# Layer 0 of a two-layer diffusion trunk: two of 24 modulation chunks made by ScalarE and GpSimd instead of TensorE

## The chip, the cores and the metric

The kernel runs on one core of one Trainium2 chip. Its time is the device time of one execution in microseconds (us), and a version's time is the median of its runs. TensorE (PE) multiplies matrices, VectorE (DVE), ScalarE (ACT) and GpSimd (POOL) work on tiles of 128 partitions, and SyncE (SP) issues the loads. Each engine runs its own list of instructions in a fixed order and waits on semaphores.

## The reference

Two streams of 256 tokens with 2048 features pass through two layers: the latent stream h, modulated by c, and the context stream hc, modulated by c_ctx. Everything is float32. What matters here is layer i = 0, with a pooling mixer:

```python
ml = (silu_c @ w_mod[i] + b_mod[i]).reshape(B, 6, 1, D)
mc = (silu_cc @ w_mod[i] + b_mod[i]).reshape(6, 1, 1, D)
...
a_lat = modulate(rms_norm(h, norm1_g[i]), ml[:, 0], ml[:, 1])
y_lat = pool_mix(a_lat, ...)
h = h + ml[:, 2] * y_lat
h = h + ml[:, 5] * conv_ffn(modulate(rms_norm(h, norm2_g[i]), ml[:, 3], ml[:, 4]), ...)
```

The same is done for hc with mc. `silu_c @ w_mod[i]` is a product of one vector per stream with a matrix of 2048 x 12288, so the weights are read for two columns only. `ml[:, 5]` and `mc[:, 5]`, the second gate, multiply what the FFN adds, and are needed last of the six.

## The kernel before

**Data.** Features lie on partitions, 128 at a time (16 tiles k), and the tokens of both streams side by side in 512 columns. A matrix product in float32 is made as three passes of a rounded type: high part times high part, high times low, low times high. ScalarE makes the high part of a weight tile (L173, a cast) and VectorE the low part (L175, a subtraction).

**Modulation.** The 12288 columns of layer 0 are 24 chunks of 512; chunk 4*which + q holds quarter q of vector number `which`, so 20 to 23 are the second gate. `mod_pe` (L231) makes a chunk on TensorE in four steps; each step loads two tiles of 512 KB, and the matmuls of L247 use the weights as the moving operand and the two condition columns as the stationary one (32 columns wide, four such groups side by side). Then ScalarE copies the result out of PSUM (L263, `modev`), four transposes (L270, `modt`) turn it, VectorE reduces it (L272) and adds the bias (L221). Chunks 22 and 23 (`LATER`) are made otherwise, on VectorE, during the FFN (`mod_pairs`): weight times condition plus sum (L315), and at the end a transpose within blocks of 32 (L325), a reduction (L326) and a small matmul that adds up the quarters (L205, `quarter_sum`). A result of chunk 20 or later is first read in the FFN's down product (L980).

**Stages.** The mixer works in four groups g of four feature tiles, and the first part of the FFN is interleaved with it: `partial(g)` multiplies the tiles of group g with the first eight column blocks f of the gate and up weights (L780 to L782, tiles `cg` and `cu`), and VectorE adds each product to a sum (L796, `part`). The shift of `modulate` goes in as a small product `pwg` or `pwu` of the raw weights with the shift columns `sh` (L759), which is copied out, transposed (L801) and reduced. The operand of group g, `Ad`, is made by ScalarE (L713) and VectorE (L714) from the mixer's output `hl`, `hc`, which is made from the mixer's matmuls `pm` (L637 to L639) by ScalarE (L701) and VectorE (L703); the sum of squares for the second norm is collected beside it (L356, L362; `n2q`, `n2acc`).

**Order.** `partial(g)` calls `between(half)` 32 times, before and inside each product. There `need(n)` advances the generator `mods()`, one step of a modulation chunk at a time (for group g the chunks g, 4+g, 8+g, 16+g, 12+g; after the last group 20 and 21), and `next(mix)` advances the mixer of the next group. In group 3 there is no mixer left; at its half 3 the second norm is closed (`n2.diagonal`, L406 to L414), at half 5 spread over all partitions (L422, `n2b`) and copied by ScalarE (L843), and from then on VectorE normalises (L438) and makes the operands A of the FFN proper (L449), and corrects the sums (L514).

**Loads.** All weight loads go through one queue on SP, one behind the other in the order of the program. A load takes one of a few rooms of 512 KB (`stage`): the one that the program freed first. It waits until all readers of the room's tile before are done, and everything behind it in the queue waits too. Three PSUM banks named "d" rotate among the products, the transposes and the small matmuls.

Of the kernel before, what the change touches and what calls it, by code (L numbers as in the profile page):

```python
# [10 lines left out]
F32 = mybir.dt.float32  # L11
F32R = mybir.dt.float32r
AF = mybir.ActivationFunctionType
ALU = mybir.AluOpType
AX = mybir.AxisListType
PSUM = bass.MemoryType.PSUM

P = 128
# [15 lines left out]
LEAD = 18  # L34
RATE = 20
PMAX = 30

NRH = 3
LATER = (22, 23)

LENT = {(2, 31): range(4, 12), (3, 6): range(8, 12), (3, 15): ()}

# [17 lines left out]
def kernel(ctx: ExitStack, tc: tile.TileContext, xT, cxT, wmod, wg, wu, wd, wp,  # L60
                         wq, wv, wo, vec, cc, rope, inv, strips, out):
    nc = tc.nc
# [34 lines left out]
    sc2 = main.tile([P, KT, 2], F32, name="sc2")  # L97
# [21 lines left out]
    def used(ts):  # L119

        for t, _ in ts:
            freed[keeper.pop(id(t))[0]] = tick()

    def lend(ks):

        for k in ks:
            if k not in rooms and k in freed:
                freed[k] = tick()
        rooms[:] = [r for r in rooms if r < 0 or r in ks] + [k for k in ks if k not in rooms]
# [15 lines left out]
    def load(src, cols, name):  # L145

        ts = []
        for j in range(0, cols, 1024):
            n = min(1024, cols - j)
            t = stage(f"{name}_{j}")  # L150
            with ExitStack() as behind:
                for ins in fetched[-1:] if in_turn else ():
                    behind.enter_context(tc.issue_after(ins))
                fetched.append(nc.sync.dma_start(t[:, :n], src(j, j + n)).ins)
            ts.append((t, n))
        return ts
# [31 lines left out]
    both = (0, 1)  # L188
# [40 lines left out]
    prod_of = []  # L229
# [250 lines left out]
    with ExitStack() as ph0:  # L480
        p0 = ph0.enter_context(tc.tile_pool(name="p0", bufs=1, reuse_waits="tile"))
        f0 = ph0.enter_context(tc.tile_pool(name="f0", bufs=6, reuse_waits="tile"))
# [11 lines left out]
        def act_tile(name, dt):  # L494
            return f0.tile([P, 2, 512], dt, tag="act", bufs=7, name=name)
# [61 lines left out]
        with ExitStack() as phs:  # L557
# [37 lines left out]
            def mods():  # L595

                for g in range(4):
                    for w in (0, 1, 2, 4):
                        yield from mod_pe(0, 4 * w + g, sc, f0)
                    yield from mod_pe(0, 12 + g, sc, f0)  # L600
                    shifts(g)
                for q in range(4):
                    if 20 + q not in LATER:
                        yield from mod_pe(0, 20 + q, sc, f0)

            pump0 = mods()
            done = [0]

            def need(n):
                while done[0] < n:  # L610
                    next(pump0, None)
                    done[0] += 1
# [212 lines left out]
            for g in range(4):  # L825
                if g < 3:
                    lend((range(8, KT), [*range(12, KT), *range(4)], range(8))[g])
                mix = mixer(g + 1) if g < 3 else None
                todo = [20 * g + 20 + n for n in STEPS] if g < 3 else []
                last = [14]  # L830
                F = {}
                rstd = n2.acc

                def between(half):
                    n = 20 * g + LEAD + (RATE if g < 3 else 19 - 4 * len(LATER)) * (half + 1) // 32
                    need(min(n, 20) if g == 0 and half == 4 else n)
                    if (g, half) in LENT:
                        lend(LENT[g, half])
                    if g == 3 and half == NRH:
                        n2.diagonal()  # L840
                        need(20 * g + 21)
                    if g == 3 and half == NRH + 2:
                        nc.scalar.copy(rstd, n2.spread_all(behind_of))  # L843
                        late_norm.append(rstd)
                    if todo and done[0] > todo[0] and half >= last[0] + 2:
                        last[0] = half
                        todo.pop(0)
                        next(mix)
                    k = (half - NRH) // 2 - 1
                    if g == 3 and 0 <= k < 12 and (half - NRH) % 2 == 0:  # L850
                        normalise(0, 3, h_of, both, rstd, f0, range(k, k + 1), keep=F)
                    if g == 3 and half == 24:
                        EARLY[NC] = late(NC, (0,))[0]
                    if g == 3 and half == 26:
                        spare = act_tile("nrm_spare", F32)
                        for j in range(2):
                            scaled[12 + j] = scale(0, 3, h_of, both, rstd, f0, 12 + j,
                                                   spare[:, j].rearrange("p (s t) -> p s t", s=2))
                    if g == 3 and half == 27:
                        for j in (14, 15):  # L860
                            scaled[j] = scale(0, 3, h_of, both, rstd, f0, j)

                partial(g, shs[g % 2], between)
                for n in todo:
                    need(n)
                    next(mix)
            need(97 - 4 * len(LATER))
            behind_of.clear()
            vector_behind.clear()
            nbank[0] = 0  # L870
# [833 lines left out]
```

## Time and profile before

| what | value |
|---|---|
| time, median of 3 runs | 3016.59 us |
| lowest and highest run | 3014.61 and 3019.01 us |
| profiled execution: its span | 3014.1 us |
| profiled execution: its own time | not listed apart from the span |
| PE busy | 2959.5 us, 98% of the span |
| DVE, ACT, POOL busy | 66%, 46%, 27% |
| DMA queues, share of 16 engines | 57.2% |
| mean of what HBM moved | 186 GB/s |

The profile is that of one execution, whose span is 2.5 us below the median and 0.5 us below the lowest run. Busy time counts instructions, not register or semaphore work. The stage of the change lies in the first 400 us: group 1 runs from about 155 to 245 us, group 2 from 245 to 335, group 3 from 335 to 400. A row of a timeline gives start, duration, engine, line, operation, result<-operands, count, and in brackets the idle time before it and what ended that.

### The profile page before, as it was taken

The page shows a single profiled execution, that of the slowest core. Times are in us where ns is not written, and L with a number is a line of the kernel's source. Part 1 is how long each engine was busy: PE and PEld are TensorE (multiplying, and loading weights), DVE is VectorE, ACT ScalarE, POOL GpSimd, SP SyncE. Part 2 cuts the span into 40 slices and gives each one's busy share as a digit, 9 for nine tenths or more (in the row PEclk, how much of TensorE's full clock was granted, in tenths as well). Part 3 has the DMA queues.
Part 4 walks back from the last instruction along what each step waited for, and adds up shares of the span by engine and source line. Part 5 has one row for each costly group of instructions (what it writes and reads, how often), then busy time and mean ns, then how long its engine had stood idle before and what let it go on. Part 6 is the DMA issues. An engine that isn't in the chain of part 4 may idle for free.

```text
span 3014.1 us, 40862 instructions
## 1 busy us (share of the span) xinstructions
PE 2959.5 (98%) x15068; PEld 2412.1 (80%) x15068; DVE 1998.0 (66%) x2895; ACT 1375.1 (46%) x2231; POOL 809.4 (27%) x782
## 2 busy tenths in 40 slices
PE   5999999999999999999999999999999999999998
PEld 3666678888888888888888887878788888888887
DVE  4455799657484866748576657484778666666666
ACT  4433454433333233333434534353546666566665
POOL 0000006212213031220314002020003665566665
PEclk9999999999999999999999999999999999999999
DMA  9798555565574847557472334342356566555553
GB/s 395 292 366 308 179 184 159 181 209 187 169 230 145 254 141 220 185 175 231 141 246 90 121 99 128 99 131 98 100 174 201 177 199 192 189 182 189 181 194 116
DMA packets 178935, 561.80 MB, mean 186 GB/s; under 512 B 17712, under 2 KB 22576, under 8 KB 178736
## 3 DMA queue, kind: packets, MB, share of 16 engines
q1 hardware_dynamic: 178736, 559.19, 57.2%
q8 instruction: 119, 1.95, 0.3%
q14 instruction: 80, 0.66, 0.1%
HBM read 557.03 MB, written 2.10 MB: 186 GB/s over the span
## 4 chain that ended last, share of the span: by engine, by line
PE 91%; DVE 3%; DMA 3%; POOL 1%; issue 1%; ACT 1%; SPq 0%; DVEq 0%; ACTq 0%; POOLq 0%
PE g L1186 5%; PE u L1186 5%; PE d L969 5%; PE d L967 5%; PE d L968 5%; PE d L1239 4%; PE g L902 4%; PE g L904 4%; PE g L903 4%; PE u L902 4%; PE u L904 4%; PE u L903 4%; PE g L1189 3%; PE u L1189 3%; PE d L1243 2%; PE k L1369 2%
## 5 line engine op out<-in xcount | busy, mean ns | idle before, releaser
L315 DVE SCALAR_TENSOR_TENSOR macc<-wm,sc,macc 128x512 f32<-128x512 f32 (+1 forms) x420 | 381.9, 941 | 71.5 <-DMA wm<-wmod 70.2
L981 POOL TENSOR_TENSOR hl<-hl,dy 128x256 f32<-128x256 f32 x160 | 154.1, 963 | 984.6 <-ACT dy L980 984.4
L1255 POOL TENSOR_TENSOR hl<-hl,dy 128x256 f32<-128x256 f32 x320 | 323.3, 1046 | 214.2 <-ACT dy L1253 212.0
L980 ACT ACTIVATE dy<-d,modT 128x256 f32<-128x256 f32 x320 | 133.4, 470 | 193.4 <-PE d L969 168.8
L981 POOL TENSOR_TENSOR hc<-hc,dy 128x256 f32<-128x256 f32 x160 | 133.3, 833 | 0.0
L1253 ACT ACTIVATE dy<-d,modT 128x512 f32<-128x512 f32 x160 | 104.5, 684 | 43.7 <-PE d L1243 41.2
L175 DVE TENSOR_TENSOR wd_2l<-wd,wd_2h 128x1024 fp32r<-128x1024 f32 (+1 forms) x44 | 55.9, 1275 | 91.3 <-ACT wd_2h L173 90.4
L175 DVE TENSOR_TENSOR wd_3l<-wd,wd_3h 128x1024 fp32r<-128x1024 f32 (+1 forms) x44 | 53.8, 1241 | 80.2 <-ACT wd_3h L173 79.1
L1341 POOL TENSOR_TENSOR rk<-rk,rp 128x256 f32<-128x256 f32 x16 | 15.1, 946 | 316.5 <-DVE rk L1340 223.4
L247 PE MATMUL mod<-wm,sc 128*32 128x512 f32 x704 | 88.8, 624 | 7.5 <-DMA wm<-wmod 7.4
L175 DVE TENSOR_TENSOR wd_1l<-wd,wd_1h 128x1024 fp32r<-128x1024 f32 (+1 forms) x44 | 54.8, 1248 | 47.8 <-ACT wd_1h L173 47.6
L411 POOL TENSOR_TENSOR n2v<-n2v,minus_half 128x4 f32<-128x4 f32 x1 | 1.0, 1011 | 316.0 <-DVE n2v L410 316.0
L173 ACT CAST wd_1h<-wd 128x1024 fp32r<-128x1024 f32 (+1 forms) x44 | 45.3, 1032 | 67.0 <-PE u L903 41.0
L175 DVE TENSOR_TENSOR wd_0l<-wd,wd_0h 128x1024 fp32r<-128x1024 f32 (+1 forms) x44 | 54.4, 1244 | 25.8 <-ACT wd_0h L173 25.0
L536 ACT ACTIVATE sg<-g 128x512 f32<-128x512 f32 x43 | 27.2, 632 | 95.9 <-DVE g L533 95.8
L1436 ACT ACTIVATE sb<-sb,nm 128x512 f32<-128x512 f32 x64 | 46.1, 721 | 52.8 <-DVE nm L1432 52.2
L967 PE MATMUL d<-act,wd_1h 128*128 128x512 f32 x172 | 67.0, 390 | 0.8 <-ACT dy L980 0.8
L967 PE MATMUL d<-act,wd_2h 128*128 128x512 f32 x172 | 67.0, 390 | 0.0
L968 PE MATMUL d<-act,wd_2h 128*128 128x512 f32 x172 | 66.9, 389 | 0.0
L968 PE MATMUL d<-act,wd_1h 128*128 128x512 f32 x172 | 66.9, 389 | 0.0
L967 PE MATMUL d<-act,wd_0h 128*128 128x512 f32 x172 | 66.9, 389 | 0.0
L969 PE MATMUL d<-act,wd_2l 128*128 128x512 f32 x172 | 66.7, 390 | 0.1
(1799 smaller groups left out, 9252.8 us busy)
## 6 DMA issues: line engine op xcount, KB each, us to landing
wm<-wmod SPq DMA_DIRECT2D x384, 512.0 KB, 6.5
wd<-wd SPq DMA_DIRECT2D x168, 512.0 KB, 4.4
wg<-wg SPq DMA_DIRECT2D x156, 512.0 KB, 4.7
wu<-wu SPq DMA_DIRECT2D x156, 512.0 KB, 4.7
wv<-wv SPq DMA_DIRECT2D x32, 512.0 KB, 4.2
wk<-wq SPq DMA_DIRECT2D x32, 512.0 KB, 3.8
wq<-wq SPq DMA_DIRECT2D x32, 512.0 KB, 3.8
wo<-wo SPq DMA_DIRECT2D x31, 512.0 KB, 4.0
```

Of the source, the lines that this page charges most:

```text
L175: low_of[:] = [eng.tensor_tensor(lo[:, :n], t[:, :n], hi[:, :n].bitcast(F32), op=ALU.subtract).ins]
L315: nc.vector.scalar_tensor_tensor(acc[s], v, sc2[:, k, s : s + 1], acc[s], op0=ALU.mult, op1=ALU.add)
L902: nc.tensor.matmul(ps, hi[:, c : c + P], xh, start=(k == 0), stop=False)
L903: nc.tensor.matmul(ps, hi[:, c : c + P], xl, start=False, stop=False)
L904: ins = nc.tensor.matmul(ps, lo[:, c : c + P], xh, start=False, stop=(k == KT - 1))
L967: nc.tensor.matmul(ps, hi[:, o : o + P], xh, start=(i == 0), stop=False)
L968: nc.tensor.matmul(ps, hi[:, o : o + P], xl, start=False, stop=False)
L969: ins = nc.tensor.matmul(ps, lo[:, o : o + P], xh, start=False, stop=(i == n - 1))
L981: nc.gpsimd.tensor_tensor(h_of(s)[:, k, :], h_of(s)[:, k, :], y[:, s], op=ALU.add)
L1186: nc.tensor.matmul(ps, hi[:, c : c + P], flat(B[k]), start=(k == 0), stop=False)
L1189: nc.tensor.matmul(ps[:, T:], lo[:, c : c + P], B[k][:, 0], start=False, stop=(k == KT - 1))
L1255: nc.gpsimd.tensor_tensor(hl[:, k, :], hl[:, k, :], y[:, q], op=ALU.add)
```

## The change

Chunks 20 and 21 leave `mods()`. A new generator `mod_beside` makes them in 16 pieces, eight for each chunk. A piece loads one tile of 512 KB (two feature tiles k of 512 columns) through the same queue and rooms; ScalarE multiplies each half with the condition of each stream (four instructions of 128x512; for stream 1 into a scratch tile `modp`, for stream 0 in place into the weight tile), and GpSimd adds the four products to the sums `beside`. Of a chunk's first half ScalarE writes the sums itself. So there are 64 instructions on ScalarE (L621, L624, L625) and 60 on GpSimd (L626, L627). After the last piece of a chunk VectorE makes two transposes and two reductions (L633, L634, tiles `modu` and `modr`), and two halves later the quarter sum goes to TensorE (L207, `modt_20s`, `modt_21s`), issued behind the last product, and VectorE adds the bias. `BESIDE` sets piece i at half 40 + 4i, counted 32g + half: chunk 20 lies in group 1 from half 8 on and in group 2 at halves 0 and 4, chunk 21 in group 2 from half 8 on and in group 3 at halves 0 and 4. The 16 loads of the two chunks in group 3 are gone there, and `need` counts eight steps fewer. The sums' tile serves later as the spare tile of the norm. Line numbers grow: L154 becomes L156, L173 L175, L247 L249, L759 L795, L780 L816, L796 L832.

```diff
+ASIDE = (20, 21)
+BESIDE = {40 + 4 * i: i for i in range(16)}
...
-                    if 20 + q not in LATER:
+                    if 20 + q not in LATER + ASIDE:
                         yield from mod_pe(0, 20 + q, sc, f0)
...
+            def mod_beside(todo):
+
+                acc = act_tile("beside", F32)
+                BESIDE_ACC.append(acc)
+                for ch in todo:
+                    for piece in range(8):
+                        g, j = divmod(2 * piece, 4)
+                        ts = load(lambda a, b: wmod[0, ch, g, :, 512 * j + a : 512 * j + b], 1024, f"wm0_{ch}_{piece}")
+                        for i in range(2):
+                            v = ts[0][0][:, 512 * i : 512 * i + 512]
+                            k = 2 * piece + i
+                            if k == 0:
+                                for s in both:
+                                    nc.scalar.activation(acc[:, s], v, AF.Copy, scale=sc2[:, k, s : s + 1])
+                                continue
+                            w = f0.tile([P, 512], F32, tag="t2", name=f"modp_{ch}_{k}")
+                            nc.scalar.activation(w, v, AF.Copy, scale=sc2[:, k, 1:2])
+                            nc.scalar.activation(v, v, AF.Copy, scale=sc2[:, k, 0:1])
+                            nc.gpsimd.tensor_tensor(acc[:, 1], acc[:, 1], w, op=ALU.add)
+                            nc.gpsimd.tensor_tensor(acc[:, 0], acc[:, 0], v, op=ALU.add)
+                        used(ts)
+                        if piece == 7:
+                            r = st.tile([P, 16, 2], F32, bufs=1, name=f"modr_0_{ch}")
+                            for s in both:
+                                t = f0.tile([P, 512], F32, tag="t2", name=f"modu{s}_0_{ch}")
+                                nc.vector.transpose(t, acc[:, s])
+                                nc.vector.tensor_reduce(out=r[:, :, s], in_=t.rearrange("p (k r) -> p k r", r=32),
+                                                        axis=AX.X, op=ALU.add)
+                            beside_sums.append((ch, r))
+                        yield
...
-                    n = 20 * g + LEAD + (RATE if g < 3 else 19 - 4 * len(LATER)) * (half + 1) // 32
+                    n = 20 * g + LEAD + (RATE if g < 3 else 19 - 4 * len(LATER + ASIDE)) * (half + 1) // 32
...
+                    if 32 * g + half in BESIDE:
+                        next(beside)
+                    if 32 * g + half - 6 in BESIDE and beside_sums:
+                        ch, r = beside_sums.pop()
+                        finish_mod(0, ch, both, quarter_sum(r, 2, f"modt_0_{ch}", prod_of))
...
-                        spare = act_tile("nrm_spare", F32)
+                        spare = BESIDE_ACC[0]
...
-            need(97 - 4 * len(LATER))
+            need(97 - 4 * len(LATER + ASIDE))
```

The order of the instructions changes with it. On SP, where group 1 passes into group 2, the queue before reads as follows (`wm_14` and `wm_3` are the modulation weights of chunks 14 and 3 on their way to TensorE, `wcg` and `wcu` weights of the gate and up products):

```order
155 L154 DMA wm_14_2_0_2088<-wmod 128x1024
156 L154 DMA wm_14_2_1024_2090<-wmod 128x1024
157 L154 DMA wm_14_3_0_2106<-wmod 128x1024
158 L624 DMA inv_2418<-inv 128x256
159 L154 DMA wm_14_3_1024_2108<-wmod 128x1024
160 L154 DMA wm_3_0_0_2137<-wmod 128x1024
161 L154 DMA wm_3_0_1024_2139<-wmod 128x1024
162 L154 DMA wm_3_1_0_2155<-wmod 128x1024
163 L154 DMA wm_3_1_1024_2157<-wmod 128x1024
```

The same place of the queue now, with what the loads wait for:

```order
162 L156 DMA wm_20_6_0_2151<-wmod 128x1024 [waits DMAHW1_49,PE_49]
163 L156 DMA wm_14_2_0_2170<-wmod 128x1024 [waits DMAHW2_49]
164 L156 DMA wm_14_2_1024_2172<-wmod 128x1024 [waits DMAHW3_49]
165 L156 DMA wm_14_3_0_2188<-wmod 128x1024 [waits DMAHW4_49,Pool_49]
166 L156 DMA wm_14_3_1024_2190<-wmod 128x1024 [waits DMAHW5_49,PE_49]
167 L156 DMA wm_3_0_0_2219<-wmod 128x1024 [waits DMAHW6_49]
168 L156 DMA wm_3_0_1024_2221<-wmod 128x1024 [waits DMAHW7_49]
169 L156 DMA wm_20_7_0_2223<-wmod 128x1024 [waits DMAHW0_49]
170 L156 DMA wm_3_1_0_2256<-wmod 128x1024 [waits DMAHW1_49]
```

Pieces 6 and 7 of chunk 20 stand in the queue, and the first tile of `wm_14_3` takes the room of piece 5 (`wm_20_5`), so it waits for GpSimd; before, the queue had no wait on GpSimd here.

On ScalarE, between the mixer's last outputs of group 1 (`pz`) and the operands of group 2 (`Ad`), now:

```order
179 L624 ACTIVATE modp_10_2007<-wm_20_5_0_2005,sc_82 128x512
180 L175 CAST wcg_0h_2143<-wcg_0_0_2139 128x1024
181 L358 ACTIVATE n2q_1980<-hc 128x256
182 L624 ACTIVATE modp_11_2012<-wm_20_5_0_2005,sc_82 128x512
183 L737 ACTIVATE pz_2036<-pm_2_2023,gbi_1707,gsc_1706 128x256 x2
184 L625 ACTIVATE wm_20_5_0_2005<-wm_20_5_0_2005,sc_82 128x512 x2
185 L358 ACTIVATE n2q_2041<-hl 128x256
186 L737 ACTIVATE pz_2058<-pm_3_2045,gbi_1707,gsc_1706 128x256 x2
187 L749 ACTIVATE Ad_2105<-hl,modT_18_2078 128x256
```

The four instructions on `wm_20_5` (L624, L625) are new in this list, and the others stand as before.

On PE, ahead of `pwg` of group 2, before (the end of `cg_2`'s product, then `pwg`):

```order
775 L782 MATMUL cg_2_2141<-Ad_2059,wcg_0bl_2078 128x512
776 L780 MATMUL cg_2_2141<-Ad_2064,wcg_0bh_2077 128x512
777 L781 MATMUL cg_2_2141<-Ad_2064,wcg_0bh_2077 128x512
778 L782 MATMUL cg_2_2141<-Ad_2064,wcg_0bl_2078 128x512
779 L759 MATMUL pwg_0_2167<-wcg_0_0_2069,sh_213 32x256
```

And now, with `modr_20` the reduced sums of chunk 20:

```order
774 L818 MATMUL cg_2_2242<-Ad_2134,wcg_0bl_2148 128x512
775 L249 MATMUL mod_3_2218<-wm_3_1_1024_2258,sc 32x512 x2
776 L249 MATMUL mod_3_2218<-wm_3_1_0_2256,sc 32x512 x2
777 L249 MATMUL mod_3_2218<-wm_3_0_1024_2221,sc 32x512 x2
778 L249 MATMUL mod_3_2218<-wm_3_0_0_2219,sc 32x512 x2
779 L207 MATMUL modt_20s<-modr_20_2235,quad 128x32
780 L795 MATMUL pwg_0_2275<-wcg_0_0_2139,sh_213 32x256
```

The matmuls of chunk 3 stood ahead of `cg_2` before; the quarter sum of chunk 20 is directly ahead of `pwg`.

On VectorE in group 3, now, from the sums' correction to the first operand A (`modT_21` is the bias add behind the quarter sum of chunk 21, which stands on PE between `n2b` and `pwg`):

```order
383 L832 TENSOR_TENSOR part_662<-part_662,cg_2_3113 128x512
384 L516 TENSOR_TENSOR part_604<-part_604,n2acc 128x512
385 L516 TENSOR_TENSOR part_633<-part_633,n2acc 128x512
386 L516 TENSOR_TENSOR part_662<-part_662,n2acc 128x512
387 L633 STREAM_TRANSPOSE modu_0_21_3107<-beside 128x512
388 L633 STREAM_TRANSPOSE modu_0_21_3110<-beside 128x512
389 L440 SCALAR_TENSOR_TENSOR nrm_3123<-hl,modT_16_521,n2acc 128x256
390 L440 SCALAR_TENSOR_TENSOR nrm_3123<-hc,modT_16_521,n2acc 128x256
391 L634 TENSOR_REDUCE modr_21_3106<-modu_0_21_3107 128x16
392 L634 TENSOR_REDUCE modr_21_3106<-modu_0_21_3110 128x16
393 L451 SCALAR_TENSOR_TENSOR A_0_3_3126<-nrm_3123,modT_12_647,A_0_3_3126 128x256 x2
394 L223 TENSOR_TENSOR modT_21_3140<-modt_21s,vt_70 32x8 x4
```

The transposes and reductions of chunk 21 are new there, and stand behind three corrections that wait for `n2b`.

More of the change, by code (lines that the diff above doesn't have):

```diff
@@ L602, in mods @@
                 for q in range(4):
-                    if 20 + q not in LATER:
+                    if 20 + q not in LATER + ASIDE:
                         yield from mod_pe(0, 20 + q, sc, f0)
+            def mod_beside(todo):
[27 more added lines that the diff above has]
+                        yield
+            BESIDE_ACC = []
+            beside_sums = []
+            beside = mod_beside(ASIDE)
             pump0 = mods()
```

## The prediction

> **What bounds the kernel now.** I read the page first, then the busy times by stage, then the chain of waits around the edges of the groups, where the change puts its work. The page's lines of engines and of the chain that ended last:
>
> ```profile
> PE 2959.5 (98%) x15068; PEld 2412.1 (80%) x15068; DVE 1998.0 (66%) x2895; ACT 1375.1 (46%) x2231; POOL 809.4 (27%) x782
> ```
>
> ```profile
> PE 91%; DVE 3%; DMA 3%; POOL 1%; issue 1%; ACT 1%; SPq 0%; DVEq 0%; ACTq 0%; POOLq 0%
> ```
>
> TensorE is the bound: 98% busy, 91% of the chain. So work taken from it counts in full, if nothing new makes it wait. Busy times by stage, in the columns span, PE, PEld, DVE, ACT, POOL (each us and instructions), granted clock, DMA share, GB/s. The rows are group 1, group 2 and group 3:
>
> ```profile
> 155.00:245.00 90.00, 87.18 (x523) 55.92 (x522) 50.99 (x105) 32.49 (x60) 0.00 (x0) 1.00 0.90 330
> 245.00:335.00 90.00, 86.24 (x498) 57.10 (x497) 54.78 (x113) 32.37 (x60) 0.00 (x0) 0.98 0.83 304
> 335.00:400.00 65.00, 64.37 (x374) 43.32 (x374) 49.57 (x108) 36.25 (x72) 1.01 (x1) 1.00 0.51 168
> ```
>
> GpSimd stands nearly idle in all three and ScalarE is half free, so the averages speak for the change. Group 3, from which the work goes, has TensorE full (64.37 of 65). But the averages hide two things: groups 1 and 2 are where the loads are densest (0.90 and 0.83 of the DMA engines), and TensorE waits there only at the group's edge.
>
> **What leaves TensorE.** All matmuls and transposes of chunks 20 and 21 lie between 354 and 400 us:
>
> ```profile
> L247 PE MATMUL mod<-wm,sc 128*32 128x512 f32 x64 | 7.9, 600 | 0.0
> ```
>
> ```profile
> L270 PE MATMUL modt<-ident,modev 128*128 128x128 f32 x8 | 1.2, 271 | 0.0
> ```
>
> That is 9.1 us by durations, which overlap at their ends. A run of 32 such matmuls of another chunk, as the timeline has it, takes 3.64 from start to end:
>
> ```profile
> 239.86 3.64 PE L247 MATMUL mod<-wm,sc 128*32 128x512 f32 x32
> ```
>
> Two of them are 7.3, and with some 1.0 of the transposes I take 8.3 us. The stage is full, so I count -8.3. Their sixteen loads leave a queue that is half idle (0.51) and count as nothing; the one wait that may go with them is this:
>
> ```profile
> PE cu L782 <- DVE wcu_4l L175: 0.5, 1, 0.5
> ```
>
> It hangs on a weight tile that stands behind those loads, so -0.5. What is late next there is VectorE, with 49.57 of 65 us, below TensorE.
>
> **What is added, by price.** The nearest rows for ScalarE's products, GpSimd's sums, VectorE's transposes and reductions and the quarter sums:
>
> ```profile
> L263 ACT COPY modev<-mod 128x512 f32<-128x512 f32 x21 | 12.3, 584 | 45.7 <-PE mod L247 45.6
> ```
>
> ```profile
> L362 POOL TENSOR_TENSOR n3q<-n3q,n3q 128x512 f32<-128x512 f32 x11 | 15.8, 1434 | 10.7 <-ACT n3q L356 7.4 <-issue 3.0
> ```
>
> ```profile
> L325 DVE STREAM_TRANSPOSE modu<-macc x36: 659/682/705, 480.4 to 1617.3; 128x512 f32<-128x512 f32 x36
> L326 DVE TENSOR_REDUCE modr<-modu x36: 633/662/675, 482.8 to 1619.2; 128x16 f32<-128x512 f32 x36
> ```
>
> ```profile
> L205 PE MATMUL modt_22s<-modr,quad x4: 178/226/274, 486.8 to 1619.4; 128*128 128x32 f32 x2, 128*128 128x16 f32 x2
> ```
>
> A piece costs ScalarE 4 x 0.58 = 2.3 us, or less where steps overlap (below); GpSimd 4 x 1.43 = 5.7; a chunk's end costs VectorE 2 x 0.68 + 2 x 0.66 = 2.7 and TensorE 0.25. ScalarE's 64 (37 us) and GpSimd's 60 (86 us) spread over some 180 us and fit. So it is not the load of an engine that decides but four places at which someone waits for them.
>
> **Place one: from group 1 to group 2.** The chain of waits there, before, then the queue of SP, and ScalarE's list (the run of 32 matmuls above is TensorE there, chunk 14):
>
> ```profile
> 243.82 10.47 DMA wcu<-wu
> 254.31 1.06 ACT wcu_0h L173
> ...
> 257.27 1.09 PE pwg L759 x16
> ...
> 258.80 0.23 PE cg L781
> ```
>
> ```profile
> 229.76 14.02 SPq L154 DMA_DIRECT2D wm<-wmod  x7
> 243.82 1.31 SPq L154 DMA_DIRECT2D wcu<-wu  x2
> ```
>
> ```profile
> 237.89 0.58 ACT L263 COPY modev<-mod 128x512 f32<-128x512 f32 x1
> 238.35 1.04 ACT L701 ACTIVATE pz<-pm,gbi,gsc 128x256 f32<-128x256 f32 x2
> ```
>
> SP's queue stood still for 14 us, because rooms were not free; loads at the edge land late, and `pwg` ran at 257.27, held by a load. Now the queue also holds a load of chunk 20 in about every eighth place, and the first tile of step 3 of chunk 14 waits for GpSimd's sums on piece 5. ScalarE's four products of that piece stand behind the `modev` copy, among a cast and the `pz`: they end at about 239, 240.7, 242.1 and 242.6, so GpSimd, at 1.43 each, ends the last sum at about 245.0. Starts 0.46 apart (237.89 and 238.35) bring Ad 4 x 0.46 = 1.8 us later. Behind the load that waits, the queue holds the other tile of step 3, two tiles of chunk 3 and piece 7. Landing times and spacing:
>
> ```profile
> wm<-wmod SPq DMA_DIRECT2D x384, 512.0 KB, 6.5
> wd<-wd SPq DMA_DIRECT2D x168, 512.0 KB, 4.4
> ```
>
> ```profile
> 185.00:200.00 15.00, 15.00 (x98) 9.92 (x98) 4.99 (x12) 3.28 (x4) 0.00 (x0) 1.00 1.02 404
> ```
>
> A queue that has run empty lands its first load after 4.4 to 6.5 us; I take 5, nearer the lower, since nothing is ahead of it. At 404 GB/s 512 KB take 1.3 us. So step 3 of chunk 14 lands from 250.0 to 251.3 (TensorE had read it by 243.5), piece 7 at 250.0 + 4 x 1.3 = 255.2. Then a product 0.6, four sums 5.7, the chunk's end on VectorE 2.7 and the quarter sum 0.25: 264.5. The quarter sum stands directly ahead of `pwg`, so `pwg` runs at 264.5 in place of 257.27: +7.2, and 6.6 to 8.7 by the two landing times. TensorE itself has, behind the late tiles (251.3), half of chunk 14 and half of chunk 3 (0.9 each), some 22 products at 0.23 and four transposes to do, 251.3 + 1.8 + 5.1 + 0.6 = 258.8, so these delays, the late Ad among them, lie inside the 7.2. At the lower end, were piece 7 there early, 258.8 - 257.3 = 1.5 is left. Behind the quarter sum on TensorE everything is queued, and VectorE and ScalarE wait for its products.
>
> **Place two: the start of group 3.** Rows of TensorE, ScalarE and VectorE there:
>
> ```profile
> 344.81 1.02 PE L422 MATMUL n2b<-n2d,ones 128*128 128x512 f32 x2
> 345.76 1.09 PE L759 MATMUL pwg<-wcg,sh 128*32 128x256 f32 x16
> ```
>
> ```profile
> 345.87 0.59 ACT L843 COPY n2acc<-n2b 128x512 f32<-128x512 f32 x1 [3.26 <-PE n2b L422]
> ```
>
> ```profile
> 346.49 0.48 DVE L438 SCALAR_TENSOR_TENSOR nrm<-hl,modT,n2acc 128x256 f32<-128x256 f32 x1
> ```
>
> ```profile
> 347.29 1.89 DVE L514 TENSOR_TENSOR part<-part,n2acc 128x512 f32<-128x512 f32 x3
> ```
>
> Today `pwg` follows `n2b` at once. Now the quarter sum of chunk 21 stands between them, and its operand comes from VectorE behind three corrections that themselves need the copy of `n2b`: copy until 346.5, corrections 1.89, two transposes 1.3, two `nrm` 0.9, two reductions 1.3, the quarter sum 0.25, that is 352.1. So +6.3 on a TensorE that had nothing to wait for. GpSimd's last sum, on a piece whose load stands well ahead, would be ready at about 347.7 (products from 341.4, then four sums), before the transposes; if it were 2 us later, that would show in full. Nothing hides this wait but matmuls that the program put behind it.
>
> **Place three: from group 2 to group 3.** The chain there ran through ScalarE and VectorE:
>
> ```profile
> 325.45 0.92 ACT pz L701 x2
> 326.37 0.94 ACT wcg_0h L173
> 327.34 1.22 DVE wcg_0l L175
> ```
>
> Three products of a piece (1.4 us) stand in ScalarE's list ahead of the first Ad: +1.4, between 0 (if the low part is later anyway) and 1.8, a whole piece.
>
> **Place four: VectorE beside a busy GpSimd.** VectorE is nearly full in the last third of each mixer, first group 1, then group 2:
>
> ```profile
> 200.00:215.00 15.00, 15.00 (x101) 9.01 (x103) 14.62 (x29) 7.38 (x13) 0.00 (x0) 1.00 0.95 323
> ```
>
> ```profile
> 290.00:305.00 15.00, 15.00 (x93) 10.83 (x96) 13.48 (x27) 6.51 (x10) 0.00 (x0) 1.00 0.75 274
> ```
>
> The trace shows the same VectorE instruction in the FFN with GpSimd idle (427 to 455 us) and with GpSimd busy throughout (456 to 480 us):
>
> ```profile
> L315 DVE SCALAR_TENSOR_TENSOR macc<-wm,sc,macc 128x512 f32<-128x512 f32 x16 | 12.4, 804 | 0.0
> ```
>
> ```profile
> L315 DVE SCALAR_TENSOR_TENSOR macc<-wm,sc,macc 128x512 f32<-128x512 f32 x14 | 16.6, 1232 | 0.0
> ```
>
> That is a stretch of 1.53. A piece falls on every 90/8 = 11 us and keeps GpSimd busy for 5.7, half the time, so a full 15 us of VectorE grows by about 15 x 0.5 x 0.53 = 4. TensorE has other matmuls queued at these places, so I take +2 for both together, between 0 and 8.
>
> [...]
>
> **The sum.** -8.3 - 0.5 + 7.2 + 6.3 + 1.4 + 2 = +8.1 us on a span of 3014.1, so 3022.2. The profiled execution is 2.5 us shorter than the median, and the change acts on any execution alike, so 3016.6 + 8.1 = 3024.7. About 0.2%, 6.0 us, is what a measurement can tell from no change: faster means below 3010.6, slower above 3022.6.
>
> **The rivals.**
>
> One: only one of the two big waits is there, because piece 7 of chunk 20 lands early, or because the quarter sum of chunk 21 finds its operand. For it speaks that SP's 14 us stand before the edge, so a load could be issued earlier; against it, the list orders it behind a load that waits for GpSimd. Then 8.1 - 7.2 + 1.5 = +2.4 or 8.1 - 6.3 = +1.8: 3018.4 to 3019.0, no change.
>
> Two, on the other side: both waits are covered. It takes that the sums of piece 7 end before 255.8 and VectorE has chunk 21's end done when `n2b` is copied, that is, that the products run some 6 us ahead of my times. GpSimd's and ScalarE's free time speaks for it; the order on VectorE, with the corrections ahead, speaks against. Then -8.8 + 1.5 + 0 to 1.4: about -6.6, 3010.0. It decides where each wait falls under 1 us.
>
> Three: VectorE and GpSimd exclude each other fully. Then in the two windows above 14.62 + 15 x 5.7/11.25 = 22.2 and 13.48 + 7.6 = 21.1 must fit in 15: 7.2 + 6.1 = 13.3 over, in place of the 2. The mixers' outputs are late and TensorE waits at both edges: 8.1 - 2 + 13.3 = +19.4, 3036. Part of it would hide behind the wait at place one, so perhaps 3030 to 3036. For it speaks the stretch in the rows above; against it, that its size there was half.
>
> **How the numbers follow.** Forecast 0.52; one wait only 0.25; both covered 0.10; full exclusion 0.13. The forecast's own range is 3021 to 3030: its unknown terms lie between -0.6 and +1.5 (landing), -1.4 and +0.5 (place three), -2 and +6 (place four). About 0.06 of it falls below 3022.6. So faster takes 0.12, with a little of the case of one wait, same 0.30, slower 0.58. The range from 3010.5 to 3032 leaves out about half of the case of cover and half of that of exclusion.
>
> **What the profile after would show.** Place one: TensorE idle for 5 to 6 us ahead of the quarter sum of chunk 20, released by VectorE's reduction, and behind that GpSimd's sums on piece 7; SP's wait for GpSimd near 245. Place two: TensorE idle for 6 us between `n2b` and `pwg`. Place four: VectorE's 128x512 instructions with two tiles in SBUF longer than before where sums run. Group 3 shorter by 8 us of matmuls. The prediction is wrong if TensorE runs through both quarter sums, or if GpSimd's sum takes well under 1.4 us, or if the loads of groups 1 and 2 become late by themselves.

## The result, and the profile after

The changed kernel takes 3045.31 us (median of 4 runs, 3044.18 to 3046.83), the kernel before 3015.6 us beside it: ratio 1.0103, 95% interval 1.0092 to 1.0115. By the medians it is 29.7 us slower, by the ratio 31; forecast were 8.1, and the range ended at 3032. The profiled execution has a span of 3042.4 us.

The busy times by stage, after, in the columns of the prediction (group 1, 2 and 3 by the times of before):

```profile
155.00:245.00 90.00, 82.33 (x469) 52.30 (x470) 57.32 (x90) 38.24 (x64) 26.14 (x18) 0.98 0.91 336
245.00:335.00 90.00, 81.02 (x479) 50.78 (x478) 66.61 (x107) 45.44 (x78) 43.80 (x30) 0.98 0.79 301
335.00:400.00 65.00, 51.15 (x250) 35.20 (x248) 51.16 (x93) 35.68 (x69) 17.85 (x13) 0.87 0.41 149
```

TensorE's idle time in groups 1 and 2 rose from 6.6 to 16.7 us (180 - 87.18 - 86.24, and 180 - 82.33 - 81.02), and in the last row it is busy for 51 of 65 us. VectorE is busier by 18 us in the first two rows, though the change gives it only eight short instructions there, and it got fewer instructions done in the same time (90 in place of 105 in group 1). What TensorE waited for, from 200 to 265 us and from 345 to 380 us (total us, times, longest):

```profile
PE cu L816 <- ACT wcu_4h L175: 4.1, 1, 4.1
PE cg L817 <- DVE Ad L750: 3.1, 2, 2.3
PE cg L816 <- ACT Ad L749: 1.4, 1, 1.4
```

```profile
PE modt_21s L207 <- DVE modr L634: 8.3, 1, 8.3
PE cg L817 <- DVE Ad L750: 2.9, 2, 2.3
PE cg L816 <- ACT Ad L749: 1.3, 1, 1.3
PE n2b L424 <- DVE n2d L416: 1.1, 1, 1.1
```

The quarter sum of chunk 21 is there as forecast (8.3 for 6.3). That of chunk 20 is not: its wait, between 265 and 300 us, is

```profile
PE modt_20s L207 <- DVE modr L634: 1.3, 1, 1.3
```

The other waits at the edges are for operands that VectorE and ScalarE make in turn. `pwg` of group 2 ran at 271.1 in place of 257.3 (+13.8), and `n2b` at 367.6 in place of 344.8 (+22.8). Such a shift is known to some 3.6 us only: a second trace, of a version of the kernel before that differs from it in the FFN alone (the second run of "And VectorE relieved", below), has 253.6 and 341.2. Why VectorE is late stands in its durations. Some of its instructions before, from 170 to 350 us (count, busy us, mean ns):

```profile
L796 DVE TENSOR_TENSOR part<-part,cu 128x512 f32<-128x512 f32 x12 | 8.2, 687 | 25.7 <-PE cu L782 25.7
L659 DVE TENSOR_TENSOR ws<-ws 128x538 f32<-128x538 f32 x8 | 5.8, 719 | 0.2
...
L714 DVE SCALAR_TENSOR_TENSOR Ad<-hc,modT,Ad 128x256 fp32r<-128x256 f32 x8 | 3.8, 474 | 0.0
...
L221 DVE TENSOR_TENSOR modT<-modT,vt 128x8 f32<-128x8 f32 x10 | 1.6, 165 | 0.3
L414 DVE TENSOR_SCALAR n2d<-ident,n2v 128x128 f32<-128x128 f32 x4 | 0.9, 278 | 0.0
```

The same after, from 170 to 370 us:

```profile
L695 DVE TENSOR_TENSOR ws<-ws 128x538 f32<-128x538 f32 x8 | 9.7, 1218 | 0.2
...
L832 DVE TENSOR_TENSOR part<-part,cu 128x512 f32<-128x512 f32 x12 | 8.2, 685 | 18.2 <-PE cu L818 18.1
...
L750 DVE SCALAR_TENSOR_TENSOR Ad<-hc,modT,Ad 128x256 fp32r<-128x256 f32 x8 | 6.9, 857 | 0.0
...
L223 DVE TENSOR_TENSOR modT<-modT,vt 128x8 f32<-128x8 f32 x10 | 6.1, 611 | 0.3
...
L416 DVE TENSOR_SCALAR n2d<-ident,n2v 128x128 f32<-128x128 f32 x4 | 3.6, 959 | 0.0
```

The five rows say how to read it. `part`, which reads one operand from PSUM, is unchanged (687 and 685). One `part` started at 187.76, while a sum of GpSimd ran from 187.53 to 188.83, and took 0.69. The other four rows, all of whose tiles lie in SBUF, are longer by 0.38 to 0.68 us in the mean, and the smallest most in proportion: an addition of 8 numbers per partition takes 0.61 us for 0.17. The lengthening does not go with an instruction's size, which speaks for a wait. Not every instruction on SBUF pays: `pf` (L704, 0.69 us before and after) started at 205.49, 214.82, 223.82 and 232.41 in group 1, and no sum ran then. ScalarE's instructions keep their length too (`Ad` 0.52 us before, 0.51 after). Two timelines show it, VectorE first, then GpSimd:

```profile
345.84 1.76 DVE L364 TENSOR_TENSOR n2acc<-n2acc,n2q 128x512 f32<-128x512 f32 x1
347.52 1.50 DVE L739 TENSOR_TENSOR hl<-hl,pz 128x256 f32<-128x256 f32 x1
348.94 0.41 DVE L739 TENSOR_TENSOR hc<-hc,pz 128x256 f32<-128x256 f32 x1
```

```profile
345.20 1.85 POOL L626 TENSOR_TENSOR beside<-beside,modp 128x512 f32<-128x512 f32 x1 [0.64 <-ACT modp L624]
347.02 1.72 POOL L627 TENSOR_TENSOR beside<-beside,wm 128x512 f32<-128x512 f32 x1
```

`n2acc`, 0.68 us by itself, ends 0.6 us after the first sum; `hl`, 0.42 by itself, ends 0.3 us after the second; `hc`, with no sum beside it, takes its usual 0.41. The engines take turns in these rows, and the two VectorE instructions that came while a sum ran, with their tiles in SBUF, waited for the sum's end, up to 1.1 us (1.76 for 0.68, 1.50 for 0.42).

### The profile page after: what moved, and what is told of

It reads as the page before. It is cut to its first block, busy times and chain, and to the rows that moved or that the text cites. A ratio compares the mean times of both kernels' runs of the same rounds, so it can differ in the third digit from the quotient of the medians.

```text
span 3042.4 us, 40908 instructions
## 1 busy us (share of the span) xinstructions
PE 2961.2 (97%) x15000; PEld 2414.1 (79%) x15000; DVE 2037.0 (67%) x2907; ACT 1413.6 (46%) x2293; POOL 890.7 (29%) x842
## 4 chain that ended last, share of the span: by engine, by line
PE 92%; DVE 3%; DMA 2%; POOL 1%; ACT 1%; issue 1%; SPq 0%; DVEq 0%; ACTq 0%; POOLq 0%
PE g L1227 5%; PE u L1227 5%; PE d L1008 5%; PE d L1009 5%; PE d L1010 5%; PE d L1280 4%; PE g L945 4%; PE g L943 4%; PE g L944 4%; PE u L945 4%; PE u L943 4%; PE u L944 4%; PE g L1230 3%; PE u L1230 3%; PE d L1284 2%; PE k L1410 2%
## 5 line engine op out<-in xcount | busy, mean ns | idle before, releaser
L626 POOL TENSOR_TENSOR beside<-beside,modp 128x512 f32<-128x512 f32 x30 | 43.9, 1464 | 241.6 <-ACT modp L624 241.0
L249 PE MATMUL mod<-wm,sc 128*32 128x512 f32 x640 | 82.8, 640 | 8.3 <-DMA wm<-wmod 8.3
L175 ACT CAST wd_1h<-wd 128x1024 fp32r<-128x1024 f32 (+1 forms) x44 | 45.3, 1032 | 70.0 <-PE u L944 44.5
L1010 PE MATMUL d<-act,wd_1l 128*128 128x512 f32 x172 | 67.2, 392 | 0.0
```

The lines of the kernel that those rows point to most:

```text
L1010: ins = nc.tensor.matmul(ps, lo[:, o : o + P], xh, start=False, stop=(i == n - 1))
```

## The experiments

Theory A, which the expectations call "port", after a cause that is the author's guess and that no trace shows: each VectorE instruction with its tiles in SBUF that meets one of GpSimd's sums waits for its end, as the two did above. Theory B: SP's queue and the quarter sums wait for GpSimd's results. Theory C: the loads and ScalarE's products cost it. Each run has its own runs of the kernel before beside it (3012.7 to 3013.6 us); the changed kernel was timed with the result only, beside 3015.6. Differences are therefore taken to the kernel before of the same time, and a us or two between versions timed apart means little.

**Without the sums.** Edit: the two lines of GpSimd are gone.

```diff
-                            nc.gpsimd.tensor_tensor(acc[:, 1], acc[:, 1], w, op=ALU.add)
-                            nc.gpsimd.tensor_tensor(acc[:, 0], acc[:, 0], v, op=ALU.add)
```

> The changed kernel without GpSimd's 60 sums (so the gate of chunks 20 and 21 holds only the first feature tile's part); loads, ScalarE's products, transposes, reductions and quarter sums stay. [...] Theory B (waiting for results): what costs is that SP's queue and the quarter sums wait for sums, which goes here as well: 3014 to 3020. Theory C (loads and ScalarE): the 16 loads at new places and ScalarE's 64 products cost most: 3035 or more. [...]

Measured: 3022.55 us, ratio 1.0031 (1.0019 to 1.0042), +9.3. That lies between the range of B (to 3020) and that of C (from 3035), and by A as by B the sums' cost goes here. So both sides have a part: some 20 of the 29.7 us go with the sums, and C has the rest. One thing more changed with the edit: the scheduler, which orders the engines' lists, now puts the transposes of chunk 21 ahead of the three corrections, and TensorE waits 1.2 us for that quarter sum, not the 6.3 of the prediction. VectorE's durations are back:

```profile
L223 DVE TENSOR_TENSOR modT<-modT,vt 128x8 f32<-128x8 f32 x10 | 1.7, 166 | 0.2
L416 DVE TENSOR_SCALAR n2d<-ident,n2v 128x128 f32<-128x128 f32 x4 | 0.9, 281 | 0.0
```

**Sums that nobody reads.** Edit: the sums go to half a tile that is not read, from the scratch tile alone; ScalarE's first products and both transposes use the other half.

```diff
+                nc.gpsimd.memset(acc[:, 1], 0.0)
...
-                                    nc.scalar.activation(acc[:, s], v, AF.Copy, scale=sc2[:, k, s : s + 1])
+                                    nc.scalar.activation(acc[:, 0], v, AF.Copy, scale=sc2[:, k, s : s + 1])
...
-                            nc.gpsimd.tensor_tensor(acc[:, 0], acc[:, 0], v, op=ALU.add)
+                            nc.gpsimd.tensor_tensor(acc[:, 1], acc[:, 1], w, op=ALU.add)
...
-                                nc.vector.transpose(t, acc[:, s])
+                                nc.vector.transpose(t, acc[:, 0])
```

> As the changed kernel, with GpSimd's 60 sums of the same size at the same places, but nobody reads them: they add to a half of the tile that the transposes don't use, and both read the scratch tile, so a room is free as soon as ScalarE is done (the result of chunks 20 and 21 is not the sum). Theory A (port): VectorE meets as many sums as before, so nearly all of the cost stays, less only the 1 to 2 us of the quarter sum of chunk 20: 3038 to 3045 us, with VectorE's short instructions (0.17 and 0.47 us) at 1.0 us and more where sums run. Theory B (waiting for results): nobody waits, so as without the sums: 3014 to 3020.

Measured: 3042.21 us, ratio 1.0095 (1.0080 to 1.0110), +29.0, and VectorE's instructions are long again (first row, 0.57 us for 0.17; second row, the sums):

```profile
L223 DVE TENSOR_TENSOR modT<-modT,vt 128x8 f32<-128x8 f32 x9 | 5.1, 565 | 0.2
```

```profile
L627 POOL TENSOR_TENSOR beside<-beside,modp 128x512 f32<-128x512 f32 x30 | 44.1, 1470 | 229.0 <-ACT modp L625 227.9
```

In this trace no engine but GpSimd waits for one of GpSimd's sums between 155 and 400 us, and the quarter sum of chunk 21 waits about as long as in the kernel without sums, since the transposes stand ahead of the corrections here too:

```profile
PE modt_21s L207 <- DVE modT L223: 1.4, 1, 1.4
```

What mainly lies between these two kernels is thus that sums run: 19.7 us. A holds for the main cost, and B falls as its explanation: without any wait for the sums the time is 29.0 us above before, with them 29.7. B had looked strong in the trace of the changed kernel, where SP waited for GpSimd for 82 us in all:

```profile
SPq L156 <- POOL beside L627: 82.0, 12, 15.4
```

But TensorE waited for a load between 120 and 380 us only once, for 0.8 us before 200.

**The quarter sum of chunk 21 later.**

```diff
-                    if 32 * g + half - 6 in BESIDE and beside_sums:
+                    if (32 * g + half - 6 in BESIDE and g < 3 or (g, half) == (3, 16)) and beside_sums:
```

> The changed kernel with only the quarter sum of chunk 21 moved from half 6 to half 16 of group 3, so that it stands well behind its operand and no longer ahead of the first pwg. If the wait of 8.3 us on it in the trace is a cost by itself: 3045.3 - 8 = 3037 us. If VectorE is late there anyway and TensorE would wait at the next instruction that needs it: 3042 to 3045.

Measured: 3038.39 us, ratio 1.0083 (1.0066 to 1.0100), 4.5 to 6 us under the changed kernel (25.2 above its before for 29.7, or by the two ratios 0.0020). That is nearer to the 3037 of a cost by itself, but the intervals overlap (from 1.0092 to 1.0100), so the size is loose. In the trace the 8.3 us are gone, and a wait of 4.3 us for `dy` has come at the FFN's down product, which the changed kernel does not have: part of the gain was taken back further on.

**Smaller sums.** Each sum as four of 128x128.

```diff
+                            for o in range(0, 512, 128):
+                                nc.gpsimd.tensor_tensor(acc[:, 1, o : o + 128], acc[:, 1, o : o + 128], w[:, o : o + 128], op=ALU.add)
...
```

> The changed kernel with each 128x512 sum of GpSimd made as four of 128x128. Theory A (port): a VectorE instruction that meets a sum waits for the rest of a quarter, some 0.35 us in place of up to 1.3, so more than half of the 24 us that the port costs goes: 3024 to 3032 us. Theory B (waiting for results): GpSimd's chain gets no shorter, rather longer by the overhead of 180 more instructions: 3045 to 3055.

Measured: 3049.93 us, ratio 1.0122 (1.0107 to 1.0137): slower still, where A had expected half of the cost to go. A small sum takes 0.62 us in the mean, not a quarter of 1.46:

```profile
L627 POOL TENSOR_TENSOR beside<-beside,modp 128x128 f32<-128x128 f32 x120 | 71.0, 624 | 207.5 <-ACT modp L624 207.5
L629 POOL TENSOR_TENSOR beside<-beside,wm 128x128 f32<-128x128 f32 x120 | 71.0, 623 | 1.5 <-ACT wm L625 1.5
```

So GpSimd is busy for 142 us in place of 87.5. VectorE waits less at a time (`ws` of 128x530 took 0.91 us between 200 and 232, for 1.22), but the results come late: VectorE's transposes wait 6.7 us in all for GpSimd's last sums, and both quarter sums make TensorE wait. Here what B names did cost:

```profile
PE modt_20s L207 <- DVE modr L636: 6.7, 1, 6.7
```

```profile
PE modt_21s L207 <- DVE modr L636: 10.5, 1, 10.5
```

**Copies in place of sums.** One input each.

```diff
-                            nc.gpsimd.tensor_tensor(acc[:, 1], acc[:, 1], w, op=ALU.add)
+                            nc.gpsimd.tensor_copy(acc[:, 1], w)
...
```

> The changed kernel with GpSimd's sums made into copies of the scratch tile and of the weight tile into the sums' tile (so the gate holds the last feature tile only): as many instructions on the same tiles, one input each. [...] If only two inputs at a time collide with VectorE: 3020 to 3025, near the 3022.6 without sums.

Measured: 3034.78 us, ratio 1.0074 (1.0060 to 1.0087), 12 us above the kernel without sums. A copy takes half as long as a sum, and costs somewhat more than half:

```profile
L626 POOL COPY beside<-modp 128x512 f32<-128x512 f32 x30 | 23.0, 768 | 266.6 <-ACT modp L624 266.2
L627 POOL COPY beside<-wm 128x512 f32<-128x512 f32 x30 | 20.8, 693 | 20.5 <-ACT wm L625 14.7 <-DMA wm<-wmod 4.5 <-POOL beside L626 0.7
```

VectorE's short instructions are longer beside the copies: an addition of 8 numbers per partition took 0.57 us at 220.94, where a copy ran from 220.88 to 221.50, and 0.16 at 213.30, where none did. So a copy, with one input, held VectorE up too. How much of the 12 us that is stays open: this kernel also waited once for a load, for 6.6 us, and 7.4 us for the quarter sum of chunk 21, for 1.2 without sums.

**The same sums at quiet places.**

```diff
-BESIDE = {40 + 4 * i: i for i in range(16)}
+BESIDE = [6, 9, 12, 15, 18, 36, 39, 42, 45, 48, 66, 69, 72, 75, 78, 81]
...
-                    if 32 * g + half - 6 in BESIDE and beside_sums:
+                    if 32 * g + half in (52, 92) and beside_sums:
```

> The changed kernel with the 16 pieces at the first two thirds of groups 0, 1 and 2 (halves 6 to 18, 4 to 16 and 2 to 17, three apart) and the quarter sums at half 20 of group 1 and half 28 of group 2, so nothing of it at the edges of the groups; as many sums of the same size. Theory A (port, and it counts only where VectorE is on the path): VectorE has 5 us of work in 15 at these places, so most of the cost goes: 3014 to 3022 us. If each sum costs the same wherever it is: 3038 to 3045.

Measured: 3025.51 us, ratio 1.0044 (1.0030 to 1.0058), +12.8: 17 us better than at the edges with as many sums, and 3.5 above the range of A. The loads, the products and the quarter sums moved with the sums, and the 8.3 us of waiting for the quarter sum of chunk 21 went too, so the 17 us are not the sums' alone. The result fits that sums cost where VectorE is on the path; at some of these places it still is, since TensorE waits 3.1 us for VectorE's Ad.

**The chunks not made at all.** Their gate is a constant.

```diff
-BESIDE = {40 + 4 * i: i for i in range(16)}
+BESIDE = {}
...
+                    if (g, half) == (3, 6):
+                        for ch in ASIDE:
+                            modT[0, ch] = mod_tile(0, ch)
+                            nc.vector.memset(modT[0, ch], 1.0)
...
```

> Chunks 20 and 21 are not made at all (their gates are a constant 1): no loads, no products, no sums, no matmuls. It is the most that any way of making them elsewhere could give. If TensorE's 8.3 us in group 3 count in full, as the forecast had it: ratio 0.997, about 3005 us. If VectorE bounds the stretch behind group 3 (it is busy for 14.4 to 15 of 15 us from 385 to 400 and from 430 to 445 in the kernel before) and TensorE waits there for what it saved: ratio 0.999 to 1.000, 3011 to 3013.

Measured: 3008.67 us, ratio 0.9987 (0.9978 to 0.9996), -4.0, between the two expectations. So there is little more than 4 us to win in this kernel by making these chunks elsewhere. TensorE's 8.3 us do go. The FFN's down product begins 13.7 us earlier in the trace (428.1 for 441.8); 3.5 of them lay before `n2b` already (341.3 for 344.8) and are within what two traces of the kernel before differ by, so the stretch from there is 10.2 us shorter. But then TensorE waits, between 420 and 470 us (this kernel, then the one before):

```profile
PE d L1012 <- ACT dy L1025: 4.3, 1, 4.3
```

```profile
PE d L967 <- ACT dy L980: 0.8, 1, 0.8
```

`dy` stands on ScalarE behind an activation that waits for VectorE, and VectorE (the fourth number behind the window) has no room there, in the kernel before:

```profile
430.00:445.00 15.00, 15.00 (x68) 12.43 (x67) 15.00 (x22) 6.84 (x9) 0.00 (x0) 1.00 0.54 169
```

**And VectorE relieved.** The sums for chunks 22 and 23 left out but for the first tile, in the kernel without chunks 20 and 21 and in the kernel before.

```diff
-                        else:
+                        elif (l, ch) not in ((0, 22), (0, 23)):
                             nc.vector.scalar_tensor_tensor(acc[s], v, sc2[:, k, s : s + 1], acc[s],
```

> Chunks 20 and 21 not made at all, and VectorE's sums for chunks 22 and 23 left out too but for the first tile (so their gate holds only that part). If VectorE's queue behind group 3 took back the gain, TensorE's 8.3 us now count in full: 8 us under the next kernel, and no wait for dy. If TensorE's gain is only 4 us for another reason, 4 under it.

> The kernel before, with VectorE's sums for chunks 22 and 23 left out but for the first tile. TensorE waits little in that stretch in the kernel before (0.8 us for dy), so 0 to 2 us less than before.

Measured: 3001.85 us (0.9965, 0.9951 to 0.9978) and 3010.45 us (0.9991, 0.9983 to 1.0000). Now the same removal is worth 8.6 us (7.8 by the two ratios), and neither trace shows the wait. The intervals are too wide to tell 8.6 from 4.0 by themselves, but together with the traces, in which the wait of 4.3 us goes with VectorE's sums, they say that VectorE's queue behind group 3 took back about half of the gain.

**Loads alone.** Without the sums and ScalarE's products but for the first tile, and then with the quarter sum of chunk 21 later too.

```diff
-                            w = f0.tile([P, 512], F32, tag="t2", name=f"modp_{ch}_{k}")
-                            nc.scalar.activation(w, v, AF.Copy, scale=sc2[:, k, 1:2])
-                            nc.scalar.activation(v, v, AF.Copy, scale=sc2[:, k, 0:1])
-                            nc.gpsimd.tensor_tensor(acc[:, 1], acc[:, 1], w, op=ALU.add)
-                            nc.gpsimd.tensor_tensor(acc[:, 0], acc[:, 0], v, op=ALU.add)
```

> The changed kernel with the 16 loads at their new places and with the transposes, reductions and quarter sums, but without GpSimd's sums and without ScalarE's products except the four of each chunk's first tile (so the gate of chunks 20 and 21 holds only that part). Without the sums alone the kernel still took 9.3 us more than before, where the forecast's other terms gave about 0. If ScalarE's 60 products at the edges of the groups cost that: 3013 to 3016 us here, 7 or more below. If the loads at their new places cost it, or the gain on TensorE isn't there at all: 3020 to 3023, as with the products.

> The kernel with the loads alone (no products but the first tile's, no sums), and the quarter sum of chunk 21 moved from half 6 to half 16 of group 3. That kernel took 10 us more than the one without the chunks. If half of it is pwg behind that quarter sum (TensorE waited 2.3 and 1.8 us there): 3014 to 3015 us, 4 less. If it is the loads: 3018 to 3019, unchanged.

Measured: 3018.69 us (1.0018, 1.0009 to 1.0027) and 3023.85 us (1.0037, 1.0023 to 1.0051). ScalarE's products are worth 3 to 4 us, less than the first expectation had it, and the intervals with and without them overlap; the loads and the chunks' ends are 10 us above the kernel without the chunks. The second expectation failed both ways: with the later quarter sum the kernel is 4 to 6 us slower. In that trace, from 345 to 372 and from 420 to 475 us:

```profile
PE pwg L790 <- issue: 4.6, 1, 4.6
```

```profile
PE d L1003 <- ACT dy L1016: 8.0, 1, 8.0
```

`pwg` waits even so: the copy of its operand `sh` has moved behind the corrections in VectorE's order (it ran at 351.45, `pwg` at 351.72). And the wait for `dy` grew. About 4 of the 10 us are the two waits at group 3, of 1.8 and 2.3 us, which go with the order of VectorE's list; that order shifts with every edit, and the edit here did not isolate it. The other 6 lie before `n2b` (347.5 for 341.3 without the chunks), and their cause stays open.

**VectorE alone, at the quiet places.** One instruction per tile and stream multiplies and adds; ScalarE and GpSimd do nothing.

```diff
...
-                            nc.gpsimd.tensor_tensor(acc[:, 0], acc[:, 0], v, op=ALU.add)
+                                    nc.vector.scalar_tensor_tensor(acc[:, s], v, sc2[:, k, s : s + 1], acc[:, s],
+                                                                   op0=ALU.mult, op1=ALU.add)
...
```

> Chunks 20 and 21 made by VectorE alone, one instruction per tile and stream that multiplies and adds (64 of them, 0.74 us each), at the quiet places (first two thirds of groups 0, 1 and 2), quarter sums in mid-group; no products on ScalarE, no sums on GpSimd. If the port made those places cost 12.8 us, most of it goes: 3008 to 3014 us, down to the 4 us of gain that leaving the chunks out altogether gave. If the loads at these places, or VectorE's 45 us, cost it: 3018 to 3026, as with GpSimd.

Measured: 3019.57 us, ratio 1.0026 (1.0015 to 1.0036), +6.0: in the second of the two ranges. It is the best of the versions that take the chunks from TensorE and still make them, and slower than the kernel before, which none of them beats.

## Why the prediction was wrong

The step that failed is place four, "VectorE beside a busy GpSimd", with +2 between 0 and 8. It measured 19.7 us. The row behind it was read wrongly: L315 at 1232 ns for 804 was taken as a stretch of 1.53, to be applied to VectorE's busy time. It was a wait, of 0.43 us in the mean, behind GpSimd instructions half the size of these sums (`hl`, `hc`, 128x256): from 471.84 us six of L315 took 6.96 us, one in 1.16, and from 472.48 GpSimd's started 1.15 us apart. With waits of up to 1.1 us behind a sum, as in the two timelines, it is the short ones in a chain that pay, and those are the steps at the groups' edges: `modT`, `hl`, Ad, `n2acc`, `n2d`. A ratio hides this; a row of a short instruction beside a busy GpSimd would have shown it. The third rival had the two engines exclude each other, with 0.13, and priced it by how much work fits into two full windows (+19.4 in all, 3036), not by the chains.

In the trace the two engines took turns by whole instructions (`n2acc` ended 0.6 us after the sum that it met, `hl` 0.3 us), and additions that read one operand from PSUM were untouched (687 and 685 ns). The prediction saw the rows of L315, and took a share of the time from them in place of turns.

The runs stand in a row that adds up to the result, each to its own before: without the chunks -4.0, with the loads and the chunks' ends +6.0, with ScalarE's products +9.3, with sums that nobody reads +29.0, the changed kernel +29.7. In their traces `n2b` ran at 341.3, 347.5, 352.4, 370.6 and 367.6 us.

What left TensorE, -8.3: wrong in what it is worth. The matmuls cost that (8.6 with VectorE relieved), but the stage behind takes half back, so -4.0. The text asked what is late next and answered with the mean of group 3, 49.57 of 65; the next bound stood 30 us behind it, where VectorE was busy for 15 of 15 us.

Place one, +7.2: the edge lost 13.8 by `pwg`, but not as argued. SP did wait for GpSimd, and the quarter sum of chunk 20 held TensorE for 1.3 us only, since everything ahead of it was later still. `pwg` ran at 255.3 without the chunks, at 259.1 with the loads, 263.4 with the products and 271.1 with the sums.

Place two, +6.3: 8.3 in the trace, of which 4.5 to 6 show in the time. The order on VectorE is the argued one: GpSimd's last sum ended at 368.8, and the transposes stood behind the corrections until 373.6. Where the scheduler put them ahead, the wait was 1.2 and 1.4 us.

Place three, +1.4: ScalarE's products at all places are worth 3 to 4 us; that they lie on the chain at this edge was not tried by itself. A product took 0.72 us, not the 0.58 of the row that priced it.

That the direction came out right is in part luck. It rested on places one and two, and with the 1.3 us of the first in place of 7.2 the same sum gives +2.2, which the prediction calls no change.

## What to carry to other kernels

The idle GpSimd was not free here, where VectorE makes what the bound engine waits for: sums that nobody read cost 19.7 us. In a case like it, count the VectorE instructions with tiles in SBUF, on the chain, that GpSimd's work will meet, and charge each a wait, here up to 1.1 us behind a sum, not a percentage. Before counting work taken from a full engine as gain, look for the next stretch in which another engine is at 100%, even in a later stage; the quickest test is to leave the work out altogether and time that. And where a scheduler orders the lists, an edit that looks local moves waits elsewhere, so read the order after each.

## What the runs showed of the hardware

Two waits of TensorE cost more than their length here. In the kernel without sums it waited 4.2 us for `dy` at the FFN's down product, from 454.8 to 459.0; the chain behind it, in start and pitch:

```profile
459.51 0.37 PE d L1007
459.89 0.42 PE d L1008
460.31 0.43 PE d L1006
...
462.87 0.28 PE d L1006
463.16 0.23 PE d L1007
```

From 459.5 to 462.9 the matmuls come about 0.43 us apart in place of 0.23, which adds some 1.5 us. The kernel without the chunks has a wait of 4.3 us there, 3.5 longer than in the kernel before (0.8). If as many slow steps or more stand behind it, which is an estimate, that makes 5 us or more, for 4.9 us that the gain lost in the trace: the down product took 1191.5 us from the start of its first matmul to that of its last, and 1186.6 before. In the changed kernel the granted clock (the last number but two) fell furthest around the quarter sum of chunk 21, where TensorE waited 8.3 us:

```profile
365.00:380.00 15.00, 5.60 (x28) 2.86 (x27) 14.11 (x26) 2.20 (x5) 3.72 (x3) 0.71 0.12 46
```

In finer stretches of that trace the clock was 1.00 from 360 to 371 us, 0.50 from 372 to 380 and 1.00 from 382 to 384. TensorE waited from 368.7 to 377.0; behind the wait a matmul of `pwg` took 0.63 us for 0.38 in the kernel before, and those of `cg` started 0.43 us apart from 380.03 to 381.31 and 0.23 apart from 381.62 to 383.01. No term of the prediction allowed for slow matmuls behind a wait.

A GpSimd sum took 1.26 us at the least for 512 columns (the changed kernel) and 0.45 for 128 (the kernel with small sums), so four small ones took 1.8 at the least; by these two figures some 0.18 us of a sum are an estimate of its fixed part.
